# Four of 44 large loads issued by GpSimd as 126 + 2 partitions, after a transfer of 7, in a store-bound q·kᵀ kernel

## Chip, cores and metric

The kernel runs on one core of a Trainium2 chip. The metric is device time of one execution in microseconds (us), as the median of several runs.

## The reference

```python
def setup_inputs():
    batch, n_heads, seq, head_dim = 8, 12, 1024, 64
    return {
        "q": np.random.randn(batch, n_heads, seq, head_dim).astype(np.float32) * 0.1,
        "k": np.random.randn(batch, n_heads, seq, head_dim).astype(np.float32) * 0.1,
    }

def reference(q, k):
    return np.einsum('bhid,bhjd->bhij', q, k).astype(np.float32)
```

There are 96 heads. Each reads 0.5 MB of q and k and writes a 1024 x 1024 float32 matrix of 4 MB, so the kernel reads 50 MB and writes 403 MB.

## The kernel before

Heads are worked on in blocks; the blocks from the fourth on hold 8 heads. Each of those has four input pieces (numbers 0 and 2 from q, 1 and 3 from k) of 128 partitions x 8 KB. There are 11 such blocks, so 44 large pieces. GpSimd casts a piece to float16, TensorE transposes and multiplies, ScalarE (ACT) and VectorE (DVE) move the products from PSUM to an output tile, and SyncE (SP) stores it as 128 partitions x 32 KB.

```python
        def load(self, n, eng, raw=None):
            if raw is None:
                x_sb = in_pool.tile([P, self.elems], F32, tag="x")
                raw = x_sb
            self.raw[n] = raw
            start = (self.first + n // 2 * self.G) * S
            src = (qf, kf)[n % 2][start : start + self.G * S]
            pin(eng.dma_start(out=raw, in_=src.rearrange("(p r) d -> p (r d)", p=P)))
...
        def scores(self, n, side):
...
            pin(
                nc.sync.dma_start(
                    out=of[self.first + n].rearrange("(p t) j -> p (t j)", p=P),
                    in_=o_sb.rearrange("p t j -> p (t j)"),
                )
            )
...
    def refill(i):                       # blocks from the fifth on
        b = blocks[i] if i < len(blocks) else None
        c = blocks[i + 1] if i + 1 < len(blocks) else None
...                                      # GpSimd casts pieces 0 to 2 of b
        yield
        if b:
            b.load(3, nc.scalar)
            b.cast(3)
        if c:
            c.load(0, nc.scalar)
            c.load(1, nc.scalar)
        yield
        yield
        if c:
            c.load(2, nc.scalar)
```

The cuts are marked with "...". All large loads but two are issued by ACT; GpSimd issues no transfer at all.

## Time and profile before

| | |
|---|---|
| time, median of 3 runs | 1070.64 us (1070.57 to 1070.69) |
| span of the profiled run | 1069.1 us |
| busy: PE, DVE, ACT, GpSimd (POOL) | 70%, 47%, 45%, 9% |
| mean transfer rate | 424 GB/s |

Three costly groups of the kernel before follow, then the two sorts of large transfers. A group's columns are: line, engine and operation, output and input with shapes, count; then busy us and mean ns of one; then the engine's idle time just before these instructions and what ended most of it. A transfer's columns are: issuer, count, KB each, median us from issue to landing.

```profile
L128 PE MATMUL ps<-kT,qT 64*128 64x512 f16 x1536 | 666.5, 618 | 253.3 <-ACT o_sb L132 226.9
L132 ACT COPY o_sb<-ps 128x1024 f32<-128x1024 f32 x480 | 475.0, 1013 | 551.5 <-DMA out_dram<-o_sb 310.7
L130 DVE COPY o_sb<-ps 128x1024 f32<-128x1024 f32 x288 | 353.1, 1227 | 498.4 <-DMA out_dram<-o_sb 364.7
...
out_dram<-o_sb SPq DMA_DIRECT2D x96, 4096.0 KB, 34.1
...
x_sb<-in_q_dram ACTq DMA_DIRECT2D x20, 1024.0 KB, 29.6
```

Read it from the end of the chain: PE waits for ACT's evictions, while ACT and DVE wait for output tiles that a store must free (310.7 and 364.7 us). Every compute engine waits for the stores, so only the DMA engines' work counts. The prediction shows the further lines.

### The profile page before, as it was taken

How to read it: one execution, taken by the hardware profiler on the slowest of the kernel's cores; microseconds unless marked ns; L12 is line 12 of the kernel's file. 1: busy time of each engine (PE TensorE's matmuls, PEld its weight loads, DVE VectorE, ACT ScalarE, POOL GpSimd, SP SyncE). 2: the span in 40 equal slices, each digit the busy share in tenths (PEclk: the TensorE clock that was granted, in tenths of full speed). 3: DMA queues.
4: the chain of work that ended last, by engine and by line, in shares of the span. 5: the costliest groups of instructions: out<-in, count | busy, mean ns of one | idle time of the engine just before them, and what ended most of it. 6: DMA issues, size and time to landing. Idle time of an engine off the chain costs nothing.

```text
span 1069.1 us, 6245 instructions
## 1 busy us (share of the span) xinstructions
PE 752.0 (70%) x2304; PEld 270.0 (25%) x2304; DVE 506.9 (47%) x384; ACT 476.3 (45%) x481; POOL 91.6 (9%) x62
## 2 busy tenths in 40 slices
PE   7774976775785786677587678668668769767740
PEld 2231322321221232232122223223123223222210
DVE  4664743542652563354265356337336537433420
ACT  4442553453444444344345445435444545544530
POOL 3202020020020020002002002000100200000000
PEclk9765555555555555555555555555555555555555
DMA  9999999999999999999999999999999999999996
GB/s 391 419 407 426 433 429 433 427 429 433 429 432 430 432 432 424 437 428 432 429 429 425 431 432 430 421 436 431 424 425 434 429 432 431 432 432 433 431 431 265
DMA packets 21920, 453.40 MB, mean 424 GB/s; under 512 B 2432, under 2 KB 2432, under 8 KB 3968
## 3 DMA queue, kind: packets, MB, share of 16 engines
q1 hardware_dynamic: 14976, 406.85, 88.8%
q10 hardware_dynamic: 6912, 46.14, 10.4%
q8 instruction: 18, 0.29, 0.1%
q14 instruction: 14, 0.11, 0.0%
HBM read 50.33 MB, written 402.65 MB: 424 GB/s over the span
## 4 chain that ended last, share of the span: by engine, by line
DMA 76%; PE 15%; ACT 4%; POOL 1%; DVE 1%; issue 0%; ACTq 0%; SPq 0%; POOLq 0%
DMA out_dram<-o_sb 70%; PE ps L128 12%; ACT o_sb L132 4%; DMA x_sb<-in_k_dram 3%; DMA x_sb<-in_q_dram 2%; PE t_ps L103 2%; POOL half_sb L88 1%; DVE o_sb L130 0%; DMA early<-in_q_dram 0%; DVE qT L115 0%; DVE kT L115 0%; ACTq L132 0%; SPq L75 0%; POOLq L88 0%; SPq L136 0%
## 5 line engine op out<-in xcount | busy, mean ns | idle before, releaser
L128 PE MATMUL ps<-kT,qT 64*128 64x512 f16 x1536 | 666.5, 618 | 253.3 <-ACT o_sb L132 226.9
L132 ACT COPY o_sb<-ps 128x1024 f32<-128x1024 f32 x480 | 475.0, 1013 | 551.5 <-DMA out_dram<-o_sb 310.7
L130 DVE COPY o_sb<-ps 128x1024 f32<-128x1024 f32 x288 | 353.1, 1227 | 498.4 <-DMA out_dram<-o_sb 364.7
L128 PEld LDWEIGHTS <-qT 64*128 64x128 f16 x1536 | 196.9, 135 | 657.2 <-issue 649.8
L88 POOL CAST half_sb<-x_sb 128x2048 f16<-128x2048 f32 x44 | 82.2, 1893 | 766.7 <-PE t_ps L103 547.7
L103 PE MATMUL t_ps<-ident,half_sb 128*128 128x128 f16 x768 | 97.8, 307 | 29.3 <-POOL half_sb L88 29.3
L115 DVE COPY qT<-t_ps 128x1024 f16<-128x1024 f16 x48 | 110.6, 2304 | 13.7 <-PE t_ps L103 13.7
L103 PEld LDWEIGHTS <-half_sb 128*128 128x128 f16 x768 | 73.1, 140 | 106.5 <-issue 73.6
L115 DVE COPY kT<-t_ps 128x1024 f16<-128x1024 f16 x48 | 58.3, 1215 | 16.0 <-PE t_ps L103 16.0
L88 POOL CAST half_sb<-early 128x512 f16<-128x512 f32 (+1 forms) x12 | 8.7, 755 | 5.6 <-DMA early<-in_q_dram 5.3
L132 ACT ACT_TABLE_LOAD x1 | 1.3, 1283 | 7.8 <-DMA early<-in_q_dram 7.8
masks.py:199 POOL TENSOR_SCALAR_AFFINE_SELECT ident<-ident 128x128 f16<-128x128 f16 x1 | 0.3, 292 | 0.1
masks.py:197 POOL MEMSET ident<- 128x128 f16 x1 | 0.2, 204 | 0.3 <-POOLq L225 0.3
L225 POOL MEMSET const-float32-0.0<- 128x1 f32 x1 | 0.1, 98 | 0.2 <-issue 0.2
L225 POOL MEMSET const-bfloat16-1.0<- 128x1 bf16 x1 | 0.1, 101 | 0.0
L225 POOL MEMSET const-uint8-127<- 128x1 uint8 x1 | 0.1, 101 | 0.0
L225 POOL MEMSET const-float32-1.0<- 128x1 f32 x1 | 0.1, 98 | 0.0
## 6 DMA issues: line engine op xcount, KB each, us to landing
out_dram<-o_sb SPq DMA_DIRECT2D x96, 4096.0 KB, 34.1
x_sb<-in_k_dram ACTq DMA_DIRECT2D x22, 1024.0 KB, 18.7
x_sb<-in_q_dram ACTq DMA_DIRECT2D x20, 1024.0 KB, 29.6
x_sb<-in_q_dram SPq DMA_DIRECT2D x2, 1024.0 KB, 11.5
early<-in_q_dram SPq DMA_DIRECT2D x4, 256.0 KB, 5.0
early<-in_k_dram ACTq DMA_DIRECT2D x4, 256.0 KB, 5.2
early<-in_q_dram SPq DMA_DIRECT2D x2, 512.0 KB, 7.4
early<-in_k_dram ACTq DMA_DIRECT2D x2, 512.0 KB, 8.0
```

Source lines behind the costliest of these rows:

```text
L88: nc.gpsimd.tensor_copy(out=self.halves[n % 2][:, :, n // 2], in_=self.raw[n].rearrange("p (r d) -> p r d", d=D),)
L103: pin(nc.tensor.transpose(t_ps[:, t], rows, ident))
L115: pin(nc.vector.tensor_copy(out=dst, in_=src))
L128: pin(nc.tensor.matmul(ps[:, js], qT[cs, g, t], kT[cs, g, js]))
L130: pin(nc.vector.tensor_copy(out=o_sb[:, t], in_=ps))
L132: pin(nc.scalar.copy(out=o_sb[:, t], in_=ps))
L225: nc = _bacc.Bacc("TRN2", target_bir_lowering=False, num_devices=1)
```

## The change

The intent, as far as the code tells it, is to shift load rows away from some of the 16 DMA engines; the prediction works out how. GpSimd takes over the issue of load 2 of four blocks; 40 large pieces stay as they were.

```diff
-        def load(self, n, eng, raw=None):
+        def load(self, n, eng, raw=None, parts=((0, P),)):
...
-            pin(eng.dma_start(out=raw, in_=src.rearrange("(p r) d -> p (r d)", p=P)))
+            src = src.rearrange("(p r) d -> p (r d)", p=P)
+            for lo, hi in parts:
+                pin(eng.dma_start(out=raw[lo:hi], in_=src[lo:hi]))
...
     make_identity(nc, ident)
+    aside = consts.tile([P, 1], F32)
+    pin(nc.gpsimd.dma_start(out=aside[:7], in_=qf[:7, :1]))
...
-        if c:
+        if c and i in (4, 6, 8, 10):
+            c.load(2, nc.gpsimd, parts=((0, 126), (126, P)))
+        elif c:
             c.load(2, nc.scalar)
```

## The prediction

> **What bounds the kernel now.** I read, in this order: the slices of the page, the queues, the chain that ended last, the windows at the end, the start of GpSimd, and then the DMA packet records of the trace one by one, because no view separates the 16 DMA engines.
>
> The slices of the page (DMA is the busy share of all 16 DMA engines in tenths) and the queues:
> ```profile
> POOL 3202020020020020002002002000100200000000
> ...
> DMA  9999999999999999999999999999999999999996
> GB/s 391 419 407 426 433 429 433 427 429 433 429 432 430 432 432 424 437 428 432 429 429 425 431 432 430 421 436 431 424 425 434 429 432 431 432 432 433 431 431 265
> ...
> q1 hardware_dynamic: 14976, 406.85, 88.8%
> q10 hardware_dynamic: 6912, 46.14, 10.4%
> q8 instruction: 18, 0.29, 0.1%
> q14 instruction: 14, 0.11, 0.0%
> ...
> DMA out_dram<-o_sb 70%; PE ps L128 12%; ACT o_sb L132 4%; DMA x_sb<-in_k_dram 3%; DMA x_sb<-in_q_dram 2%; PE t_ps L103 2%; POOL half_sb L88 1%; DVE o_sb L130 0%; DMA early<-in_q_dram 0%; DVE qT L115 0%; DVE kT L115 0%; ACTq L132 0%; SPq L75 0%; POOLq L88 0%; SPq L136 0%
> ```
> The DMA engines are full from the first loads to the end, at about 430 GB/s; no compute engine is (PE is busy 70%). 403 MB of the 453 are stores. So the time is the DMA work, and only the last slice shows slack. The windows of the end (after the engines: granted clock, DMA share, GB/s):
> ```profile
> 1040.00:1050.00 10.00, 0.00 (x0) 0.00 (x0) 0.00 (x0) 0.00 (x0) 0.00 (x0) 0.50 0.99 426
> 1050.00:1055.00 5.00, 0.00 (x0) 0.00 (x0) 0.00 (x0) 0.00 (x0) 0.00 (x0) 0.50 0.96 413
> 1055.00:1060.00 5.00, 0.00 (x0) 0.00 (x0) 0.00 (x0) 0.00 (x0) 0.00 (x0) 0.50 0.62 269
> 1060.00:1069.10 9.10, 0.00 (x0) 0.00 (x0) 0.00 (x0) 0.00 (x0) 0.00 (x0) 0.50 0.12 51
> ```
> Idle share times length is 0.04 x 5 + 0.38 x 5 + 0.88 x 9.1 = 10.1 us: the mean DMA engine is done 10 us before the end, and a few **late engines** hold it.
>
> Who they are comes from the packet records. A packet starts within a few ns of the end of the one before it on its DMA engine, and each engine's share of a transfer ends with a 4-byte record, so the packets can be threaded into 16 sequences. From 20.4 us of the span on, every sequence comes out with exactly 768 store rows of 32 KB and 328 load rows of 8 KB, with no idle gaps. All engines therefore move the same bytes, but they finish apart (us of the span; the engines' numbers are not in the trace, so I use letters):
> ```
> A 1067.3  no large fetches, but 18 ns lost on the mean store row, all along
> B 1064.6  three fetches of 16 KB (q8)      C 1063.8  five of 8 KB (q14)
> D 1062.6  three of 16 KB                   six engines 1059.3-1061.0, two of 16 KB each
> one engine 1059.9, six of 8 KB             five engines 1053.5-1055.0, at most one of 8 KB
> ```
> So the imbalance is instruction fetches (some 3 us for a 16 KB one, (1060 - 1053.7) / 2, with what it delays around it), and one engine, A, that is slower for a reason I can't see. The span ends 1.8 us after A's last record.
>
> **What the Trainium skill says.** "DMA: Bandwidth & Descriptors", section "Why a DMA increments its semaphore by 16 and not by 1": a transfer is split over the largest k of at most 16 engines that divides its partition count; on GpSimd's path, for k under 16, these are k consecutive engines from a round-robin cursor. But it names an exception: some direct copies from GpSimd use all 16 with the partitions rounded up for each. For the loads of before, k = 16 agrees with the equal 328 rows; nothing here shows the cursor. The same page, "Issuing engines are not separate DMA queues": transfers from any issuer end on the same 16 engines, so moving a load to GpSimd gives no bandwidth; the 424 GB/s mean for SP and ACT together agrees. "Runtime: NRT & Kernel Launch", "Instruction fetch mechanics": refills in blocks of 16 KiB, 256 instructions. PE's 4608 instructions make 18 blocks, and q8 has 18 packets: it agrees for PE. "SBUF — State Buffer", the box on DVE blocking DMA: GpSimd writes descriptors itself and can be held up by VectorE. Here nothing waits for that, as worked out below.
>
> **The change part by part.** *Four q loads split 126 + 2.* The diff's i = 4, 6, 8, 10 are load 2 of blocks 5, 7, 9 and 11. Before, each engine moved 8 rows of 8 KB. 126 = 14 x 9, so k = 14 with 9 rows each; the 2 go to two engines, one row each. The *7 partitions* set the cursor: 7, then 14 takes it round to 5, then 2 brings it back to 7 (7 + 14 + 2 = 23 = 16 + 7). So if the cursor starts at 0, the same two engines, 5 and 6, are left out of all four large parts. A load row takes 309 ns and the next starts 3 ns early: 306 ns. The two **spared engines** save 4 x 7 x 0.306 = 8.6 us; the 14 others gain 4 x 1 x 0.306 = 1.2 us. Bytes are the same. The point of the change is thus to unload two late engines.
>
> *Issue by GpSimd instead of ACT.* An ACT issue takes 0.33 us, so four are 1.3 us off ACT, which waits 310.7 us for stores anyway: nothing. On GpSimd the issue comes right after its last cast of the block: at about 422.28 + 1.89 = 424.2 us, where ACT issued at 426.49. The data are cast some 57 us later (the casts come every 87 us, 394.77 + 87 = 482), against a landing time of 29.6 us. So neither descriptor writing of a few us nor a wait for VectorE reaches the end.
> ```profile
> 394.77 5.57 POOL L88 CAST half_sb<-x_sb 128x2048 f16<-128x2048 f32 x3 [59.67 <-PE t_ps L103]
> 422.28 1.89 POOL L88 CAST half_sb<-x_sb 128x2048 f16<-128x2048 f32 x1 [21.94 <-DMA x_sb<-in_k_dram]
> ...
> 426.49 0.33 ACTq L75 DMA_DIRECT2D x_sb<-in_q_dram  x1
> ```
> *The transfer of 7 partitions* moves 28 bytes. It stands before the first cast on GpSimd, which now idles 2.89 us there:
> ```profile
> 1.01 0.29 POOL masks.py:199 TENSOR_SCALAR_AFFINE_SELECT ident<-ident 128x128 f16<-128x128 f16 x1
> 4.19 1.17 POOL L88 CAST half_sb<-early 128x512 f16<-128x512 f32 x2 [2.89 <-DMA early<-in_q_dram]
> ```
> An issue under 2.9 us is hidden. A longer one would delay the first store one for one, because the first store starts at 20.4 us, just as the early loads run out.
>
> *Sum.* The end is max(A, B, C, ...) after the shift, A = 1067.3. If A and B are spared: C + 1.2 = 1065.0, **2.3 us gained**. If A and another: B + 1.2 = 1065.8, **1.5 us gained**. If A isn't spared: **1.2 us lost**. It can't be more than 2.3 us, though two engines are given 8.6 us each: the third late one becomes the bound.
>
> **The rivals.** *The wrong engines are spared* (cursor not at 0, or A is neither 5 nor 6): A + 1.2, 1071.9 us. For it: the trace has no engine numbers. Against it: nobody would set the cursor with a transfer of 7 without aiming at something. *All 16 engines are used* (the exception): 126 is 15 x 8 + 6, so one engine saves 4 x 2 rows = 2.4 us and two carry 4 more rows, 1.2 us; the time is 1070.0 to 1071.9, and 1070.6 most likely, as probably neither of these is A. *GpSimd's first transfer is slow* and holds back the first casts by some us: 1071 to 1075. For it: the kernel before has no GpSimd transfer, so nothing here shows its cost. Against it: 2.9 us of slack. *ACT is freed and the kernel speeds up*: no, the DMA engines have no gaps.
>
> **Range and chances.** From 1070.64: A and B spared 1068.3 (0.25), A with another 1069.1 (0.3), A not spared 1071.9 (0.25), all 16 used 1070.6 (0.12), slow start 1073 (0.08). The middle of this lies near 1069.5, my choice. The range 1067.8 to 1072.6 takes in all but the slow start. 2% is 21 us; no part of the change reaches half of that, so within 2% gets 0.98.
>
> **What would show it.** A new GpSimd queue with 126 + 2 rows four times; two of the 16 sequences with 300 load rows on q10 and the new queue together (328 - 28) and fourteen with 332 (328 + 4). In the last windows, a shorter tail: a DMA share well above 0.12 in the last 9 us if the late engines were hit. If the idle sum of the tail stays near 10 us or grows, the wrong engines were spared. Shares of 8 rows on 15 engines would show the exception. A first cast later than 4.19 us would show the slow start. The prediction is wrong if the bytes cost more per row on GpSimd's path, if the stores lose their queued work so that engines show gaps, or if A's slowness depends on the path.

## The result

| | before | after |
|---|---|---|
| median | 1070.66 us (4 runs) | 1073.69 us (4 runs) |
| range | 1070.57 to 1071.11 | 1072.59 to 1074.38 |
| span of the profiled run | 1069.1 us | 1071.5 us |

The ratio is 1.0027, with a 95% interval of 1.0009 to 1.0044. Here and below, a ratio is the mean time of one kernel's runs over that of the other's runs of the same rounds, so it is not quite the ratio of the medians that are quoted. The change makes the kernel 3.0 us slower, and above the predicted range of 1067.8 to 1072.6.

The slices of the changed kernel, its packet count and its queues (packets, MB, share of 16 engines' time) come first, then the chain that ended last:

```profile
DMA  9999999999999999999999999999999999999995
GB/s 391 419 403 432 426 431 430 432 434 423 436 425 431 431 431 421 427 435 428 427 428 428 423 430 434 424 431 435 428 433 427 430 436 434 432 429 431 431 431 239
DMA packets 22081, 453.40 MB, mean 423 GB/s; under 512 B 2593, under 2 KB 2593, under 8 KB 4129
...
q10 hardware_dynamic: 6336, 41.95, 9.5%
q0 software_dynamic: 736, 4.20, 1.0%
...
DMA out_dram<-o_sb 70%; PE ps L130 14%; ACT o_sb L134 5%; DMA x_sb<-in_k_dram 3%; PE t_ps L105 3%; POOL half_sb L90 1%; DMA early<-in_q_dram 0%; DVE o_sb L132 0%; DVE kT L117 0%; ACTq L134 0%; SPq L77 0%; POOLq L90 0%
```

Nothing has changed in kind: the DMA engines are full to the last slice, and the stores hold 70% of the chain as before. Four megabytes have moved from ACT's queue q10 to the new queue q0.

The costly groups and the issues, as far as they are new or answer to the lines of before:

```profile
L134 ACT COPY o_sb<-ps 128x1024 f32<-128x1024 f32 x480 | 475.1, 1013 | 554.2 <-DMA out_dram<-o_sb 308.8
...
L77 POOL DMA_DIRECT2D x_sb<-in_q_dram x8 | 4.1, 520 | 1.2 <-POOL half_sb L90 1.2
L170 POOL DMA_DIRECT2D aside<-in_q_dram x1 | 0.7, 650 | 0.1
...
out_dram<-o_sb SPq DMA_DIRECT2D x96, 4096.0 KB, 34.1
...
x_sb<-in_q_dram POOLq DMA_DIRECT2D x4, 1008.0 KB, 21.2
```

ACT's wait for stores is 308.8 us instead of 310.7, its evictions take the same 1013 ns, and a GpSimd issue costs 520 ns of an engine that idles 90% of the time. Nothing is lost at the issuers.

The timeline of GpSimd at its start (start in us, length in us):

```profile
1.44 0.65 POOL L170 DMA_DIRECT2D aside<-in_q_dram  x1
4.02 1.16 POOL L90 CAST half_sb<-early 128x512 f16<-128x512 f32 x2 [1.93 <-DMA early<-in_q_dram]
```

The issue of the 7 partitions fits into the idle time: the first cast begins at 4.02 us, against 4.19 before.

The windows of the end (behind the five engines: clock, DMA share, GB/s):

```profile
1040.00:1050.00 10.00, 0.00 (x0) 0.00 (x0) 0.00 (x0) 0.00 (x0) 0.00 (x0) 0.50 1.00 429
1050.00:1055.00 5.00, 0.00 (x0) 0.00 (x0) 0.00 (x0) 0.00 (x0) 0.00 (x0) 0.50 1.02 439
1055.00:1060.00 5.00, 0.00 (x0) 0.00 (x0) 0.00 (x0) 0.00 (x0) 0.00 (x0) 0.50 0.67 288
1060.00:1071.50 11.50, 0.00 (x0) 0.00 (x0) 0.00 (x0) 0.00 (x0) 0.00 (x0) 0.50 0.11 46
```

The idle sum is 0.33 x 5 + 0.89 x 11.5 = 11.9 us, against 10.1 before. The mean DMA engine is done at 1071.5 - 11.9 = 1059.6 us instead of 1069.1 - 10.1 = 1059.0. So of the span's 2.4 us, 0.6 are a later mean, and 1.8 a longer tail: a late engine got later.

**Which engine, and where.** I threaded the packet records into 16 sequences again, as in the prediction; this is a reading of mine and not a view of the profile. Each of the four new loads shows up as 8 rows of 8 KB on 13 engines, 6 on one, and 8 + 1 on two. So 15 engines have 8 rows of the large part and one has 6, and no engine is spared. Engine A has 8 rows of each new load, as it had before. It still ends last, at 1069.5 us instead of 1067.3. The mean of the other 15 is 1059.5 instead of 1058.8. Nothing in the row counts explains A's 2.2 us. In every run, A here means the engine that ends last and has the slow store rows; whether it is the same engine on each chip is not shown.

### The profile page after: what moved, and what is told of

Read it like the earlier page. It is cut to its first block, busy times and chain, and to the rows that moved or that the text cites. A ratio compares the mean times of both kernels' runs of the same rounds, so it can differ in the third digit from the quotient of the medians.

```text
span 1071.5 us, 6257 instructions
## 1 busy us (share of the span) xinstructions
PE 755.9 (71%) x2304; PEld 271.9 (25%) x2304; DVE 507.3 (47%) x384; ACT 476.4 (44%) x481; POOL 96.3 (9%) x71
## 4 chain that ended last, share of the span: by engine, by line
DMA 74%; PE 17%; ACT 5%; POOL 1%; issue 0%; DVE 0%; ACTq 0%; SPq 0%; POOLq 0%
DMA out_dram<-o_sb 70%; PE ps L130 14%; ACT o_sb L134 5%; DMA x_sb<-in_k_dram 3%; PE t_ps L105 3%; POOL half_sb L90 1%; DMA early<-in_q_dram 0%; DVE o_sb L132 0%; DVE kT L117 0%; ACTq L134 0%; SPq L77 0%; POOLq L90 0%
## 5 line engine op out<-in xcount | busy, mean ns | idle before, releaser
L134 ACT COPY o_sb<-ps 128x1024 f32<-128x1024 f32 x480 | 475.1, 1013 | 554.2 <-DMA out_dram<-o_sb 308.8
L77 POOL DMA_DIRECT2D x_sb<-in_q_dram x8 | 4.1, 520 | 1.2 <-POOL half_sb L90 1.2
```

The lines of the kernel that those rows point to most:

```text
L77: pin(eng.dma_start(out=raw[lo:hi], in_=src[lo:hi]))
L134: pin(nc.scalar.copy(out=o_sb[:, t], in_=ps))
```

## The experiments

Each edit is shown against the changed kernel, or against the kernel before where that is said. Four labels without a b (e5 to e8) were never run by a chip; the same kernels ran as e5b to e8b.

**The theories.** ROWS: only the number of rows that the latest DMA engine moves counts, so any loss is a matter of which engines get the rows. PATH: a load that GpSimd issues costs the DMA engines more than the same load issued by ACT. COUNT: the number of transfers costs, whoever issues them.

### Taking the change apart (one chip, 5 rounds)

**e1**: the four loads by GpSimd, but whole, and no transfer of 7.

```diff
-    aside = consts.tile([P, 1], F32)
-    pin(nc.gpsimd.dma_start(out=aside[:7], in_=qf[:7, :1]))
-            c.load(2, nc.gpsimd, parts=((0, 126), (126, P)))
+            c.load(2, nc.gpsimd)
```

> The four loads are issued by GpSimd as whole 128-partition transfers, without the transfer of 7. The changed kernel was 3.0 us slower than the kernel before, and its trace shows that no DMA engine was spared (15 engines moved 8 rows of each large part, one 6, and the two odd rows went to two engines). Theory PATH: transfers issued by GpSimd cost the DMA engines something of their own, whatever their shape: 2 to 3 us slower than before. Theory SPLIT: the cost is the splitting (twice as many transfers, 9 rows on two engines): within 0.5 us of before.

Measured: 1071.54 us, before 1070.62; ratio 1.0004 (0.9992 to 1.0016). The medians are 0.9 us apart, and the interval holds 0 as well as that. Four whole loads settle nothing by themselves. (All five runs were at full TensorE clock; runs sorted by clock follow below.)

**e2**: the cut of 126 + 2, issued by ACT, and no transfer of 7.

```diff
-    aside = consts.tile([P, 1], F32)
-    pin(nc.gpsimd.dma_start(out=aside[:7], in_=qf[:7, :1]))
-            c.load(2, nc.gpsimd, parts=((0, 126), (126, P)))
+            c.load(2, nc.scalar, parts=((0, 126), (126, P)))
```

> The same split of 126 + 2 at the same four loads, but issued by ACT as before, no transfer of 7. Theory PATH: no GpSimd cost, only the shares change; if the lowest 14 engines take 9 rows each and the lowest two another row, two engines are spared 8 rows each time: either 1.2 us slower (the late engine A is among the 14) or up to 2.3 us faster (A is spared). Theory SPLIT: as slow as the changed kernel, 3 us slower.

Measured: 1072.62 us, before 1070.62; ratio 1.0013 (1.0000 to 1.0026). On ACT's queue the cut does what the prediction wanted from GpSimd: 14 engines take 9 rows each and two are left out. A is not one of the two: it has 332 rows instead of 328 and ends 1.2 us later, which is 4 x 0.306 us. The row arithmetic is therefore right for A. For the two spared engines it is not: with 8 rows fewer at each of four loads they should have ended 4 x 8 x 0.306 = 9.8 us earlier (an estimate), but their store packets became longer, and no engine ended before 1057 us, where five had ended by 1055.0 in the kernel before.

**e3**: the kernel before with only the transfer of 7 added.

```diff
-        if c and i in (4, 6, 8, 10):
+        if c and i in ():
```

> Only the transfer of 7 partitions is kept, all loads are ACT's as before. Theory QUEUE: having GpSimd's queue in the program at all costs, for example at its start: 2 us or more slower. Theory PATH: under 0.5 us, since it is one transfer of 28 bytes and its 0.65 us issue stood in idle time of GpSimd.

Measured: 1070.53 us, before 1070.62; ratio 0.9994 (0.9982 to 1.0006). No cost shows.

**e4**: the change without the transfer of 7.

```diff
-    aside = consts.tile([P, 1], F32)
-    pin(nc.gpsimd.dma_start(out=aside[:7], in_=qf[:7, :1]))
```

> The change without the transfer of 7. If the cursor decides nothing for the large part, as the changed kernel's trace suggests, this is as slow as the changed kernel, 2.5 to 3.5 us slower than before. If the cursor mattered: another pair of engines would be spared and the time would move by more than 1 us from that.

Measured: 1073.61 us (6 runs), before 1070.62; ratio 1.0025 (1.0011 to 1.0039). That is the change's own loss. The transfer of 7, said to set the cursor, decides nothing.

**How the rows were really dealt out.** The count of packets on GpSimd's queue q0 tells it from the page itself. In order: e3 (only the 7), e1 (whole loads), e4 (126 + 2, no 7), and ten transfers of 2 partitions x 4 B, which is e10 below. Each is one line of the queues:

```profile
q0 software_dynamic: 32, 0.00, 0.0%
```
```profile
q0 software_dynamic: 576, 4.19, 1.0%
```
```profile
q0 software_dynamic: 704, 4.20, 1.0%
```
```profile
q0 software_dynamic: 320, 0.00, 0.0%
```

A whole load is 128 rows and 16 records of 4 bytes: 4 x 144 = 576. If the partitions are rounded up to 16 for each part, with a small record for every missing row, the other counts follow: 7 partitions are 16 + 16 = 32, the ten small ones are 10 x 32 = 320, and a 126 + 2 load is 128 + 16 rows or fillers and 2 x 16 records, 176, four times 704. Spreading 126 over 14 engines needs no fillers: with 16 records for each part, four loads would show 4 x (128 + 32) = 640. The exception that the prediction named as a rival therefore holds for 126, 7 and 2 partitions alike.

### The dose (one chip, 5 rounds)

In e5b and e6b all ten pieces numbered 2 that ACT loaded go by GpSimd. From here on, the transfer of 7 is left out of every kernel but the unedited change; its two lines are not shown again in the diffs.

**e5b**: whole.

```diff
-        if c and i in (4, 6, 8, 10):
-            c.load(2, nc.gpsimd, parts=((0, 126), (126, P)))
+        if c:
+            c.load(2, nc.gpsimd)
```

> All ten refill loads of this kind (load 2 of blocks 4 to 13) go to GpSimd as whole transfers, instead of four. Four of them cost 0.4 us in the times (interval -0.9 to 1.7) and 0.9 us at the landing of the last store in the traces. Theory PATH (every transfer issued by GpSimd stretches store packets while it runs): 2.5 times that, 1 to 2.5 us slower than before. Theory SPLIT (only the splitting costs): 0 to 0.5 us.

Measured: 1073.00 us, before 1070.58; ratio 1.0022 (1.0008 to 1.0035). With ten loads the path alone is 2.4 us. No partition moved to another engine here, so ROWS can't explain it.

**e6b**: as 126 + 2.

```diff
-        if c and i in (4, 6, 8, 10):
+        if c:
             c.load(2, nc.gpsimd, parts=((0, 126), (126, P)))
```

> All ten as 126 + 2 by GpSimd. Four cost 2.7 us. If the cost is one per split load: 6 to 8 us slower than before. If the 2.7 us is mostly one event of the run (one unlucky stretch of the late engine A) and not a cost per load: 2 to 4 us.

Measured: 1077.22 us; ratio 1.0056 (1.0044 to 1.0069): 6.6 us.

**e7b**: only the four loads, as 112 + 16, so that each engine has exactly 7 + 1 = 8 rows and none is moved.

```diff
-            c.load(2, nc.gpsimd, parts=((0, 126), (126, P)))
+            c.load(2, nc.gpsimd, parts=((0, 112), (112, P)))
```

> Four loads by GpSimd as 112 + 16: two transfers each as in the change, but every engine gets 7 + 1 = 8 rows. If the second transfer costs (twice the descriptors and completions): as slow as 126 + 2, 2.5 to 3 us. If only the uneven shares cost: as e1, 0 to 1 us.

Measured: 1074.13 us; ratio 1.0033 (1.0020 to 1.0045): 3.5 us with no row moved. ROWS has fallen: the loss is as large as the change's without any shift of rows.

**e8b**: a probe for the order of the engines: eight loads by ACT in three parts of 112, t and 16 - t partitions.

```diff
-        if c and i in (4, 6, 8, 10):
-            c.load(2, nc.gpsimd, parts=((0, 126), (126, P)))
+        if c and 4 <= i <= 11:
+            t = 112 + (8, 4, 2, 6, 3, 5, 7, 1)[i - 4]
+            c.load(2, nc.scalar, parts=((0, 112), (112, t), (t, P)))
```

> Not for its time: load 2 of eight blocks by ACT as 112 + t + (16 - t) with t = 8, 4, 2, 6, 3, 5, 7, 1. If small transfers from ACT go to the lowest-numbered engines, one row each, the row counts 7, 8 or 9 of each of the 16 packet sequences give the number of each engine, and so where the late engines A to D stand. The time should be within 1.5 us of before, the ends of A and the others moving by their rows (0.3 us each).

Measured: one run, 1077.28 us, whose state is unknown, so its time is not used as evidence. It is a miss all the same, 6.7 us above the median of before where 1.5 was expected, although ACT issued everything; this stays unexplained. In the clean windows the engines split as the nested order demands. For t = 2 two engines have two extra rows, twelve have one and two have none; for t = 6 it is 6, 4 and 6. A has one extra row at t = 2 and two at t = 5, so it is the third, fourth or fifth in ACT's order. A cut by ACT that leaves A out must then put its whole remainder on the first two to four engines. This is why I saw no version of the idea that would beat the kernel before; none that leaves A out was run, so this is argued and not shown.

### Path or number of transfers (one chip, 5 rounds)

**e9**: the four loads as 112 + 16, by ACT.

```diff
-            c.load(2, nc.gpsimd, parts=((0, 126), (126, P)))
+            c.load(2, nc.scalar, parts=((0, 112), (112, P)))
```

> The four loads as 112 + 16 by ACT: the same two transfers and equal shares (7 + 1 rows on each engine) as in e7, which by GpSimd was 3.5 us slower than before. Theory PATH (what costs is that GpSimd issues them): within 0.7 us of before. Theory COUNT (a second transfer costs whoever issues it): about 3 us slower.

Measured: 1071.46 us, before 1071.27; ratio 1.0000 (0.9987 to 1.0012). Nothing, where GpSimd's same four cuts cost 3.5 us.

**e10**: the kernel before, with ten transfers of 2 partitions x 4 bytes by GpSimd beside its loads.

```diff
+    aside = consts.tile([P, 16], F32)
...
         if c:
             c.load(2, nc.scalar)
+            pin(nc.gpsimd.dma_start(out=aside[:2, i : i + 1], in_=qf[:2, :1]))
```

> All loads by ACT as in the kernel before; after each load 2 GpSimd issues one transfer of 2 partitions by 4 bytes, ten in all, which nobody reads. A second transfer per load cost 0.36 us each from e5 to e6 (2 rows) and 0.8 us each from e1 to e7 (16 rows). Theory FIXED (each GpSimd transfer costs by its descriptors and its completion on all 16 engines, whatever it moves): 2 to 4 us slower. Theory DATA (only the load's rows in GpSimd's queue cost): within 0.7 us of before.

Measured: 1071.48 us; ratio 1.0001 (0.9988 to 1.0015). So it isn't a fixed cost of each transfer by GpSimd, of the 2 to 4 us that FIXED expected. These transfers have 32 records each, and a whole load has 144; whether the cost goes with the bytes or with the number of rows that GpSimd has to describe was not separated.

**e11**: the change again, unedited.

> The changed kernel once more, for a narrower interval beside e9 and e10: 2.5 to 3.5 us slower than before. In its trace: the engine that ends last is A again, with 8 rows of each split load.

Measured: 1072.45 us, before 1071.27; ratio 1.0011 (0.9999 to 1.0024): only 1.2 us in this job, less than half of what was expected. All five runs were at about half clock, which turns out to matter (below).

### The last four (one chip, 5 rounds)

**e12** and **e13**: ten loads as 112 + 16, by GpSimd and by ACT. **e14**: e5b again. **e15**: the change, unedited.

```diff
-        if c and i in (4, 6, 8, 10):
-            c.load(2, nc.gpsimd, parts=((0, 126), (126, P)))
+        if c:
+            c.load(2, nc.gpsimd, parts=((0, 112), (112, P)))    # e12; nc.scalar in e13
```

> Ten loads by GpSimd as 112 + 16, so that each DMA engine has 8 rows per load, as before. Theory (GpSimd's path stretches the stores): 2.5 times the 3.5 us of four such loads, some 6 to 9 us more than before. Rival (the number of transfers, whoever issues them): the same as the ACT run beside it, whatever that is. If neither path nor number matters: 0.

> The same ten cuts of 112 + 16, issued by ACT. Theory: 0 within 1 us, as no row is moved and nothing goes by GpSimd. Rival: as much as the GpSimd run beside it, within 1 us.

> Ten uncut loads by GpSimd, as once before (+2.4 us). Theory: 2 to 3 us more than before, between the two runs of 112 + 16. Rival: 0, as no load is cut.

> The change itself, unedited, on the same chip. Theory: between 1.2 and 3 us more than before, the range of the earlier jobs, and about 4/10 of a ten-load split by GpSimd. Rival: 4/10 of the ACT run with ten cuts, plus the rows that the 126 + 2 cut moves, at most 1.2 us.

| | median, us | against 1070.84 | ratio (95%) |
|---|---|---|---|
| e12: ten, 112 + 16, GpSimd | 1078.41 | +7.6 | 1.0065 (1.0051 to 1.0079) |
| e13: ten, 112 + 16, ACT | 1072.34 | +1.5 | 1.0019 (1.0006 to 1.0031) |
| e14: ten, whole, GpSimd | 1073.22 | +2.4 | 1.0025 (1.0012 to 1.0038) |
| e15: the change | 1074.09 | +3.3 | 1.0032 (1.0019 to 1.0045) |

e12 and e14 came out as PATH expected, and COUNT as the whole explanation falls: the same cuts cost five times as much by GpSimd as by ACT (7.6 and 1.5 us by the medians; 3.4 times by the ratios), and uncut loads by GpSimd cost 2.4 us. But PATH missed e13 by half a us, as cutting has a price of its own, some 0.15 us a load, and e15 lies just above its 1.2 to 3. By the medians the two together (7.6) are more than their sum (2.4 + 1.5 = 3.9), so the cut seems dearer on GpSimd's path; by the ratios it is 7.0 against 4.7, which the intervals don't quite keep apart. Runs with four loads point the same way: e7b lost 3.5 us, e9 none and e1 0.4 to 0.9. A load cut as 112 + 16 costs 0.76 us by e12, one cut as 126 + 2 costs 0.66 by e6b; four are 3.0 and 2.6 us. This is the loss of the change.

The clock that the page grants TensorE was 0.523 in the profiled run of e12 and 1.000 in that of e13. It isn't the cause of the difference between these two: among e12's own runs those at 1.000 took 1077.18 to 1078.70 us, and those at about half clock 1076.51 and 1079.27. Each of the 9 runs of the kernel before lies between 1069.75 and 1071.54, at either clock.

**Sorted by clock.** For the change itself the clock isn't without effect. The kernel before took 1070.5 us on average at 1.000 (16 runs of the experiments' four jobs) and 1071.3 at about half clock (22 runs). The four loads as 126 + 2 by GpSimd (the change in three jobs, and e4) took 1074.9 us at 1.000 (6 runs, 1073.88 to 1076.59) and 1072.9 at half (14 runs, 1071.73 to 1074.62). So the loss is some 4.5 us at full clock and 1.7 at half; in e6b it is 7.6 and 4.4 against the runs of before at the same clock. In e11 all five runs were at half clock and lost 1.3 us against such runs of before: its small loss is no contradiction. All five runs of e1 and of e9 were at 1.000; against such runs of before they lost 1.2 and 0.2 us. GpSimd's path costs more than ACT's at either clock (e12 7.7 and 6.7 us, e13 1.5 and 2.1). This sorting was done after the fact; why the clock matters was not tried.

The end windows of e12, and then of e13, show whose work grew:

```profile
1050.00:1055.00 5.00, 0.00 (x0) 0.00 (x0) 0.00 (x0) 0.00 (x0) 0.00 (x0) 0.50 1.00 433
1055.00:1060.00 5.00, 0.00 (x0) 0.00 (x0) 0.00 (x0) 0.00 (x0) 0.00 (x0) 0.50 0.79 341
1060.00:1077.50 17.50, 0.00 (x0) 0.00 (x0) 0.00 (x0) 0.00 (x0) 0.00 (x0) 0.50 0.12 51
```
```profile
1050.00:1055.00 5.00, 0.00 (x0) 0.00 (x0) 0.00 (x0) 0.00 (x0) 0.00 (x0) 1.00 0.99 426
1055.00:1060.00 5.00, 0.00 (x0) 0.00 (x0) 0.00 (x0) 0.00 (x0) 0.00 (x0) 1.00 0.87 374
1060.00:1070.40 10.40, 0.00 (x0) 0.00 (x0) 0.00 (x0) 0.00 (x0) 0.00 (x0) 1.00 0.13 54
```

The idle sums are 0.21 x 5 + 0.88 x 17.5 = 16.4 us and 0.01 x 5 + 0.13 x 5 + 0.87 x 10.4 = 9.7 us, so the mean engine ends at 1061.1 us in e12 and at 1060.7 in e13. The spans differ by 7.1 us, but the means by 0.4. Nearly all that GpSimd's path adds is tail. The threaded packet records name the engine:

| profiled run | A ends, us | the other 15, mean |
|---|---|---|
| before | 1067.3 | 1058.8 |
| after | 1069.5 (+2.2) | 1059.5 (+0.7) |
| e15, the change again | 1072.3 (+5.0) | 1060.7 (+1.9) |
| e14, ten whole, GpSimd | 1070.8 (+3.5) | 1059.6 (+0.8) |
| e13, ten cut, ACT | 1068.5 (+1.2) | 1060.5 (+1.7) |
| e12, ten cut, GpSimd | 1076.0 (+8.7) | 1060.8 (+2.0) |

Cutting makes all engines about 1.7 us later, A not more than the rest. Going by GpSimd makes A later, and the mean of the others by less than 1 us.

**What happens on A.** A's store packets of 32 KB, in order of time, in the changed kernel around the load of 602 us (start in us of the span, and ns beyond the 1213 of an undisturbed packet; those 40 ns or more beyond it):

```
after, 585-625 us:    608.4 +786
  rows of the new load on A: 608.1, 610.7, 611.3, 613.1, 614.9, 616.7, 618.6, 620.4
before, 585-625 us:   617.0 +41, 618.5 +67
```

The one store packet that starts right behind the first row of GpSimd's load takes 2.0 us instead of 1.2. At the load before it, A moved rows at 428.7 and 430.3 us, and the store packet behind the second, at 430.6 us, was 645 ns too long. The same packet, behind the first or second row, was 862, 775 and 825 ns too long in e15 (at 254, 432 and 611 us), 640 and 781 ns in e14 and 619 and 856 ns in e12, in the two windows that I looked at in each. A second threading, of whole runs, finds five such packets on A in e12, 3.9 us together of the 8.7 that A lost. It also finds them on other engines: packets over 400 ns too long, right behind a row of GpSimd's, are 24 on the other 15 engines in e12 (1.6 each) and 9 in the changed kernel (0.6 each, against two on A). So A isn't the only engine that is hit; it is hit more often. In the kernel before, the only such excess on A in the windows of 380 to 470 and 550 to 650 us is 302 ns at 390.2 us, beside an instruction fetch of 8 KB; the changed kernel has its like, 305 ns at 387.9 us. The size fits: 645 + 786 ns are 1.4 of the 2.2 us that A lost in the changed kernel. A packet 626 ns too long at 249.6 us, where the threading is less sure, would make it 2.1. Once the GpSimd loads are over, A loses nothing more: from 770 us on, stores land a constant 2.2 us later than in the kernel before.

It isn't the whole of it. Not every GpSimd load does this to A: in e11, which lost only 1.2 us, I found it clearly at one of the three loads that I could read (553 ns). And in e4, where A ended 2.8 us later, these packets came to no more than about 0.5 us.

## Why the prediction was wrong

- **What bounds the kernel** was right. The end is the end of one DMA engine, A, in every profiled run that I threaded; no compute engine came into the end of the chain. But the change cost more at full TensorE clock than at half (some 4.5 and 1.7 us), which the prediction had no place for.
- **"126 = 14 x 9, so k = 14 with 9 rows each" is the step that failed first.** The Trainium skill ("DMA: Bandwidth & Descriptors", section "Why a DMA increments its semaphore by 16 and not by 1") has both the rule and the exception; I put the exception at 0.12. On GpSimd's path the runs show the exception, 15 x 8 + 6, in the records and in the packet counts. So no engine was spared, and the 1.5 to 2.3 us of gain were never there. The same section's order for ACT's path (the lowest-numbered k) agrees with e8b's nested counts, and e2's 14 x 9 agrees with its rule for k.
- **"Neither descriptor writing … reaches the end" was true of the issuers, and hid the second failed step**: that a row costs the DMA engines the same from either issuer. The skill's "Issuing engines are not separate DMA queues" in the same page says the transfers interleave on the same 16 engines. They do (in the threads, rows of all queues follow each other on every engine; the 424 GB/s that the prediction names is no proof of it), but not at the same cost: ten cuts by GpSimd cost 7.6 us, by ACT 1.5. This is the "bytes cost more per row on GpSimd's path" that the prediction listed as what would make it wrong, though it gave it no chance and no size. The term of the sum that was missing is 4 x 0.66 = 2.6 us by e6b, whose cut is the change's own, or 4 x 0.76 = 3.0 by e12; the change lost 3.0.
- **The rival of all 16 engines** was right in its mechanism, 1070.0 to 1071.9 us, and was off by the same missing term. Its lower end was a slip: had A been the engine with 6 rows, the prediction's own sum (A - 2.4 us) would give about 1068.2.
- **The slow first transfer** was rightly made small: the first cast came at 4.02 us, and no cost shows in e3.
- **The rows' worth**, 0.306 us each, was right for rows added to A (e2: +4 rows, 1.2 us). That an engine spared of rows ends earlier by as much, the 8.6 us of the sum, was not borne out in e2: the two spared engines did not end earlier.
- **Within 2%** was right, for the reason that was given.

**What stays open.** Why a store packet of A, right behind the first or second row of most of these GpSimd loads, takes 0.6 to 0.9 us longer is not in the trace. Nor is why A is slow to begin with, whether the two belong together, or why the change loses more at full clock. The mix of clocks in each job goes far to account for its 3.0, 3.3 and 1.2 us. A wait of GpSimd's descriptor writing for VectorE, which the prediction names, was not tested as a cause of the long packets.

## What to carry to other kernels

Where the DMA engines are full to the end, ask which single engine finishes last, and price a change on that engine; a mean over 16 hides it. Before relying on how a transfer is dealt over the engines, count its packets: fillers in the queue's line show rounding up. Moving a load to an idle issuer isn't free because the issuer is idle: here the same bytes by GpSimd cost the kernel 0.24 us for a whole load of 1 MB and 0.66 to 0.76 us for a cut one. And sort the runs by clock before comparing jobs: here the same kernel lost 1.7 or 4.5 us.

## What the Trainium skill lacked or had wrong

- "DMA: Bandwidth & Descriptors", section "Why a DMA increments its semaphore by 16 and not by 1": it says that some direct copies by GpSimd use all 16 engines, but not which. Here all that were seen did: 126, 7 and 2 partitions showed 144, 32 and 32 packets (the 126 by taking 32 for the 2 from 176). The fillers, a 4-byte record for each row missing to a multiple of 16, aren't mentioned there.
- The same page, "Issuing engines are not separate DMA queues": this section gives the issuer no cost on the DMA engines, which leads one to think that it doesn't matter to them. Ten loads cut as 112 + 16 took 7.6 us more by GpSimd and 1.5 us more by ACT (ratios 1.0065 and 1.0019); ten whole ones took 2.4 us more by GpSimd, twice.
- The same page, section "Latency and other measured facts", has DMA engines 7 and 15 usually slower than the rest and, as a best guess, puts it down to GpSimd's descriptor rings, so to GpSimd's path alone. Here engine A loses about 18 ns on each store row of 1213 ns in a kernel that has no GpSimd transfer, and it was the last in every profiled run that I threaded. In e8b it is the third to fifth in ACT's order; if that is the order of the numbers, it is neither 7 nor 15.
- "Runtime: NRT & Kernel Launch", "Instruction fetch mechanics", calls the cost of crossing a block boundary "mostly hidden". That is said of the engine that fetches; what a fetch takes from a busy DMA engine isn't given. Here a packet of 16 KB took 0.94 us (median of 18), and by the prediction's estimate it makes the DMA engine that carries it some 3 us later at the end.
